# The last four heads' keys turned to token rows behind the last output product

## The chip, the cores and the metric

The kernel runs on one core of a Trainium2 chip. The metric is the device time of one execution in microseconds; the time before is 2034.35 us, the median of three runs (2033.86 to 2036.96).

A core has five engines with instruction streams of their own: PE (TensorE) multiplies matrices and transposes, with results in PSUM banks; DVE (VectorE), ACT (ScalarE) and POOL (GpSimd) work on elements; SP (SyncE) does little but issue transfers, which 16 DMA engines carry out. Each engine takes its instructions in order. They wait for each other by semaphores.

## The reference

One step of a hybrid decoder layer. A normalised input `h` (16 meta tokens, 1024 tokens of a prompt, 32 tokens of eight samples: 1072 rows) is multiplied by one wide matrix. Its parts feed eight heads of attention (the change calls it softmax attention; the weights are made by breaking a stick) and a gated linear attention, and both go through one output product, a norm and a residual. Beside the two `y`, the new keys and values are outputs, by token:

```python
h = rms_norm(x, norm_pre_g[l])
(q, k, v), sg, (gq, gk, gv, gf), gg = branch_inputs(h, w_in[l], w_alpha[l], b_alpha[l])
o_sb = sb_prompt(q, k, v, sb_bias[l])
o_gla, s_end = gla_prompt(gq, gk, gv, gf)
x = x + rms_norm(branch_output(o_sb, sg, o_gla, gg, gla_norm_g[l], w_out[l]), norm_post_g[l])
k_p.append(k)
```

`new_k_prompt` is 1040 tokens x 8 heads x 128 features, `new_k_sample` 32 tokens x 8 heads x 128. One token's key of one head is a run of 512 bytes, and the next token's lies 4 KB further on.

## The kernel before

The input product is made by feature: 128 features of one head in the partitions, the 1072 tokens along the row, in three chunks of 384, 384 and 304 columns (`CHUNKS`, L40). All products are made of float32 split in two parts, three matmuls for one (L347 to L349). For each head, `head(h)` (L721) makes values, keys and queries, in this order, while the attention of the head before runs between them (`attend`, L689). A `Weaver` (L58) interleaves such pieces of work: a piece is a generator that is resumed after a number of beats, and the products call `W.beat()`. A scheduler then sets the order on each engine; with `tc.add_manual_dep(..., NOSYNC, reason="behind")` the kernel asks that one instruction stands behind another, with no wait.

A chunk of keys leaves PSUM in `ev_k` (L761): ACT copies it to `raw`, `split_k` makes the two parts for the attention, and `tok_out` (L548) makes token rows: three PE transposes to a bank (L556), a copy by ACT to `st` (L558 to L561), and a store from SP to the outputs (L564; for the last chunk also L566 and L567).

The output stage (L1361) works on the 1024 prompt tokens in two halves of 512 by a scheme with seven products (`p`), each for two column blocks (`q`). The last one, `p` 4 with `q` 1, runs token tile by token tile (L1744 to L1750, four tiles of 128 tokens): `before_last`, eight steps of `product` (L1679) on weights kept in SBUF, `take_last` (L1561; sum on DVE, square on ACT), and `finish1` (L1658), which makes the root and the four blocks of 512 columns of the tile's rows. `end_block` (L1648) scales, adds the input and stores from SP. For tile 3, one block goes by ACT and POOL and is stored by ACT (L1676), and block 1 is stored in two halves. The names in the views: `u` is block 0, `y` blocks 2 and 3, `og` block 1. `finish_samples` (L1630) does the 32 sample rows beside it (`held`: eight stores of 32 KB, L1646).

At this point the slots of region C (`REGION`, L1401; 10 to 13 of the 16 long slots) have held the forms of product 7 and are free, and so are the slots of the ring of weights (4 and 5). `bank` (L1513) deals six PSUM banks in turn; two more have the tag `S`. Transfers tell of their landing by eight semaphores, `DMAHW0` to `DMAHW7`, dealt in turn to the DMAs of SP and ACT together; a DMA waits until the one that had its semaphore before has landed.

Of the kernel before, what the change touches and what calls it, by code (L numbers as in the profile page):

```python
# [10 lines left out]
F32 = mybir.dt.float32  # L11
# [4 lines left out]
AF = mybir.ActivationFunctionType  # L16
# [4 lines left out]
P = 128  # L21
# [7 lines left out]
T = META + SEQ + NSMP  # L29
REAL = META + SEQ  # L30
TOUT = SEQ + NSMP
HEADS = 8
# [19 lines left out]
IDLE = -1000000  # L52

EB = 4 * P
NOSYNC = mybir.DependencyInfo(mybir.DependencyClass.NoSync, mybir.DependencyReason.DATA)


# [32 lines left out]
def hybrid_step(ctx: ExitStack, tc: tile.TileContext, x_prompt, x_sample, cache_k, cache_v, state_gla,  # L90
# [3 lines left out]
    nc = tc.nc  # L94
    mm = nc.tensor.matmul
    vec, act, pool = nc.vector, nc.scalar, nc.gpsimd
# [13 lines left out]
    dram = ctx.enter_context(tc.tile_pool(name="dram", bufs=1, space=DRAM))  # L110
# [3 lines left out]
    W = Weaver()  # L114
# [5 lines left out]
    ident = cst.tile([P, P], F32, name="ident")  # L120
# [33 lines left out]
    zd = [dram.tile([P, 256], F32, name=f"zd{b}") for b in range(NB)]  # L154
    od = [dram.tile([P, TOUT], F32, name=f"od{g}") for g in range(NK)]
    md = [dram.tile([P, TOUT], F32, name=f"md{g}") for g in range(NK)]
    znd = dram.tile([NSMP, HEADS, NSMP], F32, name="znd")
    td = [dram.tile([P, 8, 1024], F32, name=f"td{j}") for j in range(4)]
    sd = [[dram.tile([P, 512], F32, name=f"sd{j}_{k}") for k in range(8)] for j in range(2)]
# [35 lines left out]
    with tc.tile_pool(name="xp", bufs=2) as xp, tc.tile_pool(name="xps", bufs=5, space=PSUM) as xps:  # L195
        wf = xp.tile([P, 12, P], F32R, tag="wf", bufs=1, name="wf")
        wfl = [stg.tile([P, 2, P], F32R, tag="stg", name=f"wfl{kk}") for kk in range(6)]
        first = [accp.tile([P, 512], F32, tag="acc", name=f"acc_v0_{c}") for c in range(3)]
# [106 lines left out]
        for c, (lo, hi) in enumerate(XCHUNKS):  # L305
            n = hi - lo
# [173 lines left out]
    def spread(ins):  # L480

        if W.mark is not None:
            tc.add_manual_dep(ins.ins, W.mark.name, NOSYNC, reason="spread")

# [53 lines left out]
    with tc.tile_pool(name="sp", bufs=1) as sp, tc.tile_pool(name="sps", bufs=1, space=PSUM) as sps:  # L538
# [9 lines left out]
        def tok_out(raw, c, lo, hi, h, outp, outs_, nm):  # L548

            yield 6  # L550
            os_ = outs_[0].rearrange("b t h d -> (b t) h d")
            ps = sps.tile([P, 512], F32, tag="z", bufs=4, name=f"tk_{nm}_{c}")
            st = stage(f"st_{nm}_{c}")
            for i in range(3):
                r = min(P, hi - lo - i * P)
                nc.tensor.transpose(ps[:r, i * P:(i + 1) * P], raw[:, i * P:i * P + r], ident[:])  # L556
            if c < 2:
                act.copy(st[:], ps[:, :384])  # L558
            else:
                act.copy(st[:, :256], ps[:, :256])  # L560
                act.copy(st[:48, 256:], ps[:48, 256:384])  # L561
            sv = st[:].rearrange("p (a d) -> p a d", d=P)
            nt = 3 if c < 2 else 2
            nc.sync.dma_start(outp[0, 0, lo:lo + nt * P, h, :].rearrange("(a p) d -> p a d", p=P), sv[:, :nt])  # L564
            if c == 2:
                nc.sync.dma_start(outp[0, 0, 8 * P:REAL, h, :], sv[:16, 2, :])  # L566
                nc.sync.dma_start(os_[:, h, :], sv[16:48, 2, :])  # L567
# [153 lines left out]
        def head(h):  # L721
# [39 lines left out]
            def ev_k(c, ps, lo, hi):  # L761
                raw = stage(f"kraw{h}_{c}")
                act.copy(raw[:, :hi - lo], ps)
                W.spawn(split_k(raw, c, lo, hi))
                W.spawn(tok_out(raw, c, lo, hi, h, new_k_prompt, new_k_sample, f"k{h}"))
            inproj(C_SK + h * P, ev_k, 0, f"k{h}")
            qt = [sp.tile([P, SEQ], F32R, tag=f"q{i}", name=f"q{i}_{h}") for i in range(2)]
            qsm = sp.tile([P, NSMP], F32, tag="qsm", name=f"qsm{h}")
# [28 lines left out]
    with tc.tile_pool(name="gp", bufs=1) as gp, tc.tile_pool(name="gps", bufs=1, space=PSUM) as gps:  # L797
# [20 lines left out]
        def slot(c):  # L818

            return 8 if c == 8 else 4 * (1 - c % 2) + c // 2  # L820
# [540 lines left out]
    with ExitStack() as out:  # L1361
# [151 lines left out]
        def bank(nm):  # L1513
            n = next(at) % 6
            return accp.tile([P, 512], F32, tag="acc", name=nm) if n < 3 else ops.tile([P, 512], F32, tag="m", bufs=3, name=nm)
# [114 lines left out]
        def finish_samples():  # L1630
            yield 5
            ps = ops.tile([P, 512], F32, tag="S", bufs=2, name="tsp")
            tot = op.tile([P, 4], F32, tag="tot", name="tots")
            vec.tensor_tensor(tot[:, 1:2], sssm[:, 0:1], sssm[:, 1:2], ALU.add)
            mm(ps[:, 0:1], rep, tot[:, 1:2], start=True, stop=True)
            vec.tensor_copy(tot[:, 0:1], ps[:, 0:1])
            r = rstd_(op, tot[:, 0:1], D, P, 1, "ys")
            xv = x_sample.rearrange("b t d -> (b t) d")
            yv = y_sample.rearrange("b t d -> (b t) d")
            for i in range(2):  # L1640
                x = stage(f"xs_{i}")[:, :256]
                for j in range(4):
                    nc.sync.dma_start(x[32 * j:32 * j + 32], xv[:, i * 1024 + j * 256:i * 1024 + (j + 1) * 256])
                vec.scalar_tensor_tensor(ysm[i][:], ysm[i][:], r, x, ALU.mult, ALU.add)
                for j in range(4):
                    nc.sync.dma_start(yv[:, i * 1024 + j * 256:i * 1024 + (j + 1) * 256], ysm[i][32 * j:32 * j + 32])  # L1646

        def end_block(i, b, r, behind=None):  # L1648
            o = scaled[i][:] if b == 1 else sums_[4 + i, b]
            w = 256 if b == 1 and i == 3 else 512  # L1650
            for c0 in range(0, 512, w):
                cs, ys = slice(c0, c0 + w), slice(b * 512 + c0, b * 512 + c0 + w)
                ins = vec.scalar_tensor_tensor(o[:, cs], o[:, cs], r, xr[i, b][:, cs], ALU.mult, ALU.add).ins
                if behind is not None:
                    tc.add_manual_dep(ins, behind.name, NOSYNC, reason="behind")
                nc.sync.dma_start(y_prompt[0, 512 + i * P:512 + (i + 1) * P, ys], o[:, cs])

        def finish1(i, v):  # L1658
            rt = op.tile([P, 12], F32, tag="rs", name=f"rt_y{i}")
            r, t = rt[:, 0:1], rt[:, 1:2]  # L1660
            act.activation(r, v, AF.Ln)
            act.activation(r, r, AF.Exp, scale=-0.5)
            vec.scalar_tensor_tensor(t, r, v, r, ALU.mult, ALU.mult)
            vec.tensor_scalar(t, t, -0.5, 1.5, ALU.mult, ALU.add)
            vec.tensor_tensor(r, r, t, ALU.mult)
            if i == 3:
                o = sums_[7, 2]
                act.activation(o, o, AF.Copy, scale=r)
                pool.tensor_tensor(o, o, xr[3, 2], ALU.add)
            for b in (0, 3) if i > 1 else (0, 2, 3, 1):  # L1670
                end_block(i, b, r)
            if i == 2:
                end_block(i, 2, r)
                return lambda behind: end_block(i, 1, r, behind)
            if i == 3:
                nc.scalar.dma_start(y_prompt[0, 512 + 3 * P:, 1024:1536], o)  # L1676
                end_block(i, 1, r)
# [53 lines left out]
        for pair in ((1, 2), (6,), (5, 3), (7, 4)):  # L1731
            for q in range(2):
                banks = [bank(f"b{pair[0]}{q}_{t}") for t in range(4)]
                for p in pair:
# [3 lines left out]
                    if (p, q) != (4, 1):  # L1738
                        step(p, q, banks, p == pair[0], p == pair[-1])
                        AFTER.get((p, q), lambda: None)()  # L1740
        W.spawn(finish_samples())

        scaled, rest = {}, None
        for t in range(4):  # L1744
            tot = before_last(t)
            for k in range(8):
                product(banks[t], t, 4, k, kept[k], False, True)
                W.beat()
            take_last(t, banks[t], tot, rest)
            rest = finish1(t, tot[:, 1:2])  # L1750
        W.flush()


# [27 lines left out]
```

## Time and profile before

| | us |
|---|---|
| median of three runs | 2034.35 |
| the profiled execution | 2034.71 |
| its span, first to last instruction | 2033.0 |
| PE busy | 2004.2 |
| DVE busy | 1496.9 |
| ACT busy | 1018.4 |
| PE, transposes of keys `tk_k` (L556), 72 of 272 ns | 93.8 to 731.5 |
| last product of PE starts | 2023.1 |

The profile is of one execution. Its times are from the first instruction on; "start us, us" in a timeline are start and duration. Matmuls are pipelined: the next one starts before the one before has ended, so what a matmul costs in a stream is the distance between starts, not its duration. A row of the table by stretches has, in order: the stretch, its length, busy us of PE, PEld, DVE, ACT and POOL with the number of instructions, the granted clock of PE, the share of time in which the DMA engines are busy, and GB/s.

### The profile page before, as it was taken

The numbers are of one execution on the slowest core, as the hardware profiler recorded it, in microseconds if no ns is written. First come the engines' busy times: TensorE is split into PE (matmuls) and PEld (weight loads), VectorE is DVE, ScalarE is ACT, GpSimd is POOL, SyncE is SP. The second block draws the span as 40 slices with busy tenths as digits, with TensorE's granted clock in tenths as the row PEclk, the third lists the DMA queues.
The fourth block names the chain that finished last, engine by engine and source line by source line (L and its number), as shares of the span: only waits on it lengthen the run. The fifth ranks groups of instructions, "written<-read, shape, count | busy, mean of one in ns | idle before, by whom it ended". The sixth has DMA issues, their size and how long they took to land.

```text
span 2033.0 us, 41746 instructions
## 1 busy us (share of the span) xinstructions
PE 2004.2 (99%) x12379; PEld 1852.4 (91%) x12379; DVE 1496.9 (74%) x6163; ACT 1018.4 (50%) x2377; POOL 96.1 (5%) x355
## 2 busy tenths in 40 slices
PE   6999999999999999999999999999999999999998
PEld 5999999999999999999999999999988898788776
DVE  7368888888888888899898888978444338365466
ACT  7356767675766757433535335254433335343342
POOL 0111110101000010000000000000000000000000
PEclk9999999999999999999999999999999999999999
DMA  6345554545555442433342434335767656352485
GB/s 205 98 136 161 143 163 132 175 129 157 151 161 151 141 125 77 142 101 89 103 108 80 126 79 120 90 93 176 243 220 234 221 186 221 104 176 94 141 281 204
DMA packets 371980, 301.92 MB, mean 149 GB/s; under 512 B 42336, under 2 KB 312264, under 8 KB 371752
## 3 DMA queue, kind: packets, MB, share of 16 engines
q1 hardware_dynamic: 371448, 298.73, 49.1%
q8 instruction: 97, 1.59, 0.3%
q14 instruction: 131, 1.07, 0.2%
q10 hardware_dynamic: 304, 0.53, 0.1%
HBM read 241.84 MB, written 57.31 MB: 147 GB/s over the span
## 4 chain that ended last, share of the span: by engine, by line
PE 91%; DVE 3%; DMA 2%; ACT 2%; issue 1%; SPq 0%; DVEq 0%; POOL 0%; POOLq 0%; ACTq 0%
PE acc_g L347 6%; PE acc_g L348 5%; PE acc_g L349 5%; PE b L1682 4%; PE b L1683 4%; PE b L1684 4%; PE acc_gv L347 3%; PE acc_gv L348 3%; PE acc_gv L349 3%; PE acc_k L347 3%; PE acc_k L349 3%; PE acc_k L348 3%; PE acc_q L348 3%; PE acc_q L347 3%; PE acc_q L349 3%; PE acc_v L347 3%
## 5 line engine op out<-in xcount | busy, mean ns | idle before, releaser
L470 DVE SCALAR_TENSOR_TENSOR jk<-kp,qb 128x128 f32<-128x128 f32 x2048 | 593.6, 290 | 46.2 <-DMA qb<-qsd 3.0
L347 PE MATMUL acc_g<-hT,wh_g 128*128 128x368 f32 (+2 forms) x768 | 250.7, 326 | 0.0
L348 PE MATMUL acc_g<-hT,wh_g 128*128 128x368 f32 (+2 forms) x768 | 247.2, 322 | 0.0
L349 PE MATMUL acc_g<-hT,wl_g 128*128 128x368 f32 (+2 forms) x768 | 246.9, 321 | 0.0
L470 DVE DVE_READ_ACCUMULATOR jk<-kp,qb 128x1 f32 x2048 | 167.3, 82 | 0.0
L1682 PE MATMUL b<-ring,f 128*128 128x512 f32 x416 | 163.9, 394 | 1.5 <-DVE y L1547 1.1
L1683 PE MATMUL b<-ring,f 128*128 128x512 f32 x416 | 162.3, 390 | 0.0
L1684 PE MATMUL b<-ring,f 128*128 128x512 f32 x416 | 161.9, 389 | 0.0
L347 PEld LDWEIGHTS acc_g<-hT,wh_g 128*128 128x128 f32 x768 | 144.3, 188 | 12.0 <-issue 10.7
L348 PEld LDWEIGHTS acc_g<-hT,wh_g 128*128 128x128 f32 x768 | 144.4, 188 | 0.7
L349 PEld LDWEIGHTS acc_g<-hT,wl_g 128*128 128x128 f32 x768 | 144.2, 188 | 0.0
L1481 DVE TENSOR_TENSOR ring<-wr,ring 128x512 fp32r<-128x512 f32 x104 | 71.2, 689 | 97.7 <-ACT ring L1480 97.1
L1480 ACT CAST ring<-wr 128x512 fp32r<-128x512 f32 x104 | 64.0, 620 | 134.7 <-PE b L1684 78.1
L347 PE MATMUL acc_gv<-hT,wh_gv 128*128 128x402 f32 (+2 forms) x384 | 130.1, 339 | 0.0
L347 PE MATMUL acc_k<-hT,wh_k 128*128 128x384 f32 (+1 forms) x384 | 126.1, 328 | 0.0
L348 PE MATMUL acc_gv<-hT,wh_gv 128*128 128x402 f32 (+2 forms) x384 | 125.3, 326 | 0.0
L349 PE MATMUL acc_gv<-hT,wl_gv 128*128 128x402 f32 (+2 forms) x384 | 125.0, 326 | 0.0
L349 PE MATMUL acc_k<-hT,wl_k 128*128 128x384 f32 (+1 forms) x384 | 124.7, 325 | 0.0
L348 PE MATMUL acc_k<-hT,wh_k 128*128 128x384 f32 (+1 forms) x384 | 124.4, 324 | 0.0
L347 PE MATMUL acc_q<-hT,wh_q 128*128 128x368 f32 (+2 forms) x384 | 124.3, 324 | 0.0
L348 PE MATMUL acc_q<-hT,wh_q 128*128 128x368 f32 (+2 forms) x384 | 123.6, 322 | 0.0
L349 PE MATMUL acc_q<-hT,wl_q 128*128 128x368 f32 (+2 forms) x384 | 123.3, 321 | 0.0
(483 smaller groups left out, 5263.6 us busy)
## 6 DMA issues: line engine op xcount, KB each, us to landing
kp<-in_cache_k_dram SPq DMA_DIRECT2D x512, 64.0 KB
vr<-in_cache_v_dram SPq DMA_DIRECT2D x64, 512.0 KB
qb<-qsd SPq DMA_DIRECT2D x64, 256.0 KB
wr_g<-in_w_in_dram SPq DMA_DIRECT2D x64, 256.0 KB
wr<-td SPq DMA_DIRECT2D x56, 256.0 KB
tf<-in_w_out_dram SPq DMA_DIRECT2D x48, 256.0 KB
td<-tf SPq DMA_DIRECT2D x48, 256.0 KB
wr<-in_w_out_dram SPq DMA_DIRECT2D x48, 256.0 KB
```

Source lines behind the costliest of these rows:

```text
L347: mm(acc[c][:, :n], wh, hh[k][:, lo:hi], start=(k == 0), stop=False)
L348: mm(acc[c][:, :n], wh, hl[k][:, lo:hi], start=False, stop=False)
L349: W.mark = mm(acc[c][:, :n], wl, hh[k][:, lo:hi], start=False, stop=(k == NK - 1)).ins
L470: ins = vec.scalar_tensor_tensor(jk[:], kp[:], 1.0, qbs[h, b][:, t, :], ALU.mult, ALU.mult, accum_out=zt[:, t, NPG - 1 - i:NPG - i])
L1480: act.copy(wh, r)
L1481: vec.tensor_tensor(wl, r, wh.bitcast(F32), ALU.subtract)
L1682: mm(bk[:], ah, wh, start=first and k == 0, stop=False, skip_group_check=True)
L1683: mm(bk[:], ah, wl, start=False, stop=False, skip_group_check=True)
L1684: W.mark = mm(bk[:], al, wh, start=False, stop=last and k == 7, skip_group_check=True).ins
```

## The change

For heads 4 to 7 (`LATE` is 4) `ev_k` no longer starts `tok_out`. It stores `raw` as it is, by feature, to a scratch `kd` in DRAM (3 stores a head, 128 rows of 1536 or 1216 bytes). Behind the weights of the output stage, `load_late` brings the four heads back, 128 x 1072 each, to two slots of region C. `late_rows` then makes the token rows: nine banks `kb0` to `kb8` of four transposes each, two banks for a head's 1024 first tokens, and the ninth for the last 48 tokens of all four heads; all of them stand behind the last product. ACT copies six of the banks and DVE three (5, 6 and 8, behind the last block of `y`) to `kst`. SP stores a head's 1024 tokens in one DMA of 512 KB, and the last 48 tokens in two. The order on SP around the last tile's stores is asked for by hand.

```diff
+LATE = HEADS - 4
+    kd = [dram.tile([P, T], F32, name=f"kd{i}") for i in range(4)]
...
-                W.spawn(tok_out(raw, c, lo, hi, h, new_k_prompt, new_k_sample, f"k{h}"))
+                if h < LATE:
+                    W.spawn(tok_out(raw, c, lo, hi, h, new_k_prompt, new_k_sample, f"k{h}"))
+                else:
+                    nc.sync.dma_start(kd[h - LATE][:, lo:hi], raw[:, :hi - lo])
...
-                nc.sync.dma_start(y_prompt[0, 512 + i * P:512 + (i + 1) * P, ys], o[:, cs])
+                ends[:] = [ins]
+                stores.append(nc.sync.dma_start(y_prompt[0, 512 + i * P:512 + (i + 1) * P, ys], o[:, cs]).ins)
...
-            act.activation(r, r, AF.Exp, scale=-0.5)
+            tail[:] = [act.activation(r, r, AF.Exp, scale=-0.5).ins]
...
-                act.activation(o, o, AF.Copy, scale=r)
+                tail.append(act.activation(o, o, AF.Copy, scale=r).ins)
...
+        kr = [slot(REGION["C"][i], f"kr{i}") for i in range(2)]
+        kf = [kr[j // 2][:, j % 2 * T:(j % 2 + 1) * T].bitcast(F32) for j in range(4)]
+        kst = [slot(REGION["C"][2 + i], f"kst{i}") for i in range(2)]
+
+        def load_late():
+            for j in range(4):
+                yield 4
+                spread(nc.sync.dma_start(kf[j], kd[j][:]))
+
+        def late_rows():
+            last = W.mark
+            for n in range(9):
+                ps = ops.tile([P, 512], F32, tag="S", bufs=2, name=f"kb{n}") if n in (2, 3) else bank(f"kb{n}")
+                rows = P if n < 8 else T - 8 * P
+                for i in range(4):
+                    src = kf[n // 2][:, (n % 2 * 4 + i) * P:(n % 2 * 4 + i + 1) * P] if n < 8 else kf[i][:, 8 * P:T]
+                    ins = nc.tensor.transpose(ps[:rows, i * P:(i + 1) * P], src, ident[:]).ins
+                    tc.add_manual_dep(ins, last.name, NOSYNC, reason="behind")
+                st = (kst[n // 4][:, n % 4 * 512:(n % 4 + 1) * 512] if n < 8 else slot(4, "kst2")[:, 0:512]).bitcast(F32)[:rows]
+                if n in (5, 6, 8):
+                    ins, first = vec.tensor_copy(st, ps[:rows, :]).ins, ends[0]
+                else:
+                    ins, first = act.copy(st, ps[:rows, :]).ins, (last, *tail)[min(n, 2)]
+                tc.add_manual_dep(ins, first.name, NOSYNC, reason="behind")
+                if n == 8:
+                    sv = st.rearrange("p (h d) -> p h d", d=P)
+                    nc.sync.dma_start(new_k_prompt[0, 0, 8 * P:REAL, LATE:HEADS, :], sv[:16])
+                    nc.sync.dma_start(new_k_sample[0].rearrange("b t h d -> (b t) h d")[:, LATE:HEADS, :], sv[16:48])
+                elif n % 2:
+                    sv = kst[n // 4][:, n % 4 * 512 - 512:n % 4 * 512 + 512].bitcast(F32)
+                    ins = nc.sync.dma_start(new_k_prompt[0, 0, :1024, LATE + n // 2, :].rearrange("(a p) d -> p a d", p=P),
+                                            sv.rearrange("p (a d) -> p a d", d=P)).ins
+                    for a, b in {1: ((stores[-4], ins), (stores[-3], stores[-4])),
+                                 3: ((ins, stores[-3]), (stores[-2], ins), (stores[-1], stores[-2]))}.get(n, ()):
+                        tc.add_manual_dep(a, b.name, NOSYNC, reason="behind")
+
+        W.spawn(load_late())
...
+        late_rows()
```

Three places in the built programs. First SP, at the stores of tiles 0 and 1. Before (`u_0`, `y_0_0`, `y_1_0` and the first `og` are tile 0's; the second digit of `y` is the tile):

```order
L1656 DMA out_dram<-u_0_29289 128x512
L1656 DMA out_dram<-y_0_0_30310 128x512
L1646 DMA out_dram<-held_29114 32x256 x4
L1646 DMA out_dram<-held_29115 32x256 x4
L1656 DMA out_dram<-y_1_0_30627 128x512
L1656 DMA out_dram<-og_31518 128x512
L1656 DMA out_dram<-u_1_29291 128x512
```

And now, with the loads `kr`:

```order
L1651 DMA out_dram<-held_29034 32x256 x4
L1651 DMA out_dram<-held_29035 32x256 x4
L1664 DMA out_dram<-u_0_29209 128x512
L1664 DMA out_dram<-y_0_0_30230 128x512
L1664 DMA out_dram<-y_1_0_30547 128x512
L1664 DMA out_dram<-og_31443 128x512
L1757 DMA kr_31359<-kd_125 128x1072
L1757 DMA kr_31360<-kd_126 128x1072
L1664 DMA out_dram<-u_1_29211 128x512
```

All eight sample stores have moved ahead of tile 0's rows, and two loads stand between tiles 0 and 1; one more stands behind tile 1's `og`, and the first one further ahead. Second, DVE at the same place, the work that fills these stores. Before:

```order
L1653 SCALAR_TENSOR_TENSOR y_0_0_30310<-y_0_0_30310,rt_y_31523,xr_0_2_31448 128x512
L1644 SCALAR_TENSOR_TENSOR held_29114<-held_29114,vrt_ys,xs_31486 128x256
L1644 SCALAR_TENSOR_TENSOR held_29115<-held_29115,vrt_ys,xs_31496 128x256
L1653 SCALAR_TENSOR_TENSOR y_1_0_30627<-y_1_0_30627,rt_y_31523,xr_0_3_31453 128x512
L1566 TENSOR_TENSOR u_1_29641<-b_1_31239,u_1_29641 128x512
L1653 SCALAR_TENSOR_TENSOR og_31518<-og_31518,rt_y_31523,xrs_31158 128x512
```

And now:

```order
L1660 SCALAR_TENSOR_TENSOR y_0_0_30230<-y_0_0_30230,rt_y_31448,xr_0_2_31372 128x512
L1649 SCALAR_TENSOR_TENSOR held_29034<-held_29034,vrt_ys,xs_31411 128x256
L1660 SCALAR_TENSOR_TENSOR y_1_0_30547<-y_1_0_30547,rt_y_31448,xr_0_3_31377 128x512
L1660 SCALAR_TENSOR_TENSOR og_31443<-og_31443,rt_y_31448,xrs_31078 128x512
L1571 TENSOR_TENSOR u_1_29561<-b_1_31159,u_1_29561 128x512
L1649 SCALAR_TENSOR_TENSOR held_29035<-held_29035,vrt_ys,xs_31421 128x256
```

The second half of the sample rows has moved behind three instructions of 512 columns. Third, the end of the program, with the semaphores that each row waits for. SP before, from the last block of tile 2 on:

```order
L1656 DMA out_dram<-og_31610 128x512 [waits DMAHW6_49,DVE_49]
L1656 DMA out_dram<-u_3_29295 128x512 [waits DMAHW7_49,DVE_49]
L1656 DMA out_dram<-y_1_3_30633 128x512 [waits DMAHW1_49,DVE_49]
L1656 DMA out_dram<-og_31654 128x256 [waits DMAHW2_49,DVE_49]
L1656 DMA out_dram<-og_31654 128x256 [waits DMAHW3_49,DVE_49]
```

And now:

```order
L1664 DMA out_dram<-og_31538 128x512 [waits DMAHW3_49,DVE_49]
L1780 DMA out_dram<-kst_31361 128x8x128 [waits DMAHW4_49,Activation_49]
L1664 DMA out_dram<-u_3_29215 128x512 [waits DMAHW5_49,DVE_49]
L1664 DMA out_dram<-y_1_3_30553 128x512 [waits DMAHW6_49,DVE_49]
L1780 DMA out_dram<-kst_31361 128x8x128 [waits DMAHW7_49,Activation_49]
L1664 DMA out_dram<-og_31582 128x256 [waits DMAHW0_49,DVE_49]
L1664 DMA out_dram<-og_31582 128x256 [waits DMAHW1_49,DVE_49]
L1780 DMA out_dram<-kst_31362 128x8x128 [waits DMAHW2_49,DVE_49,Activation_49]
L1780 DMA out_dram<-kst_31362 128x8x128 [waits DMAHW3_49,DVE_49,Activation_49]
L1776 DMA out_dram<-kst_31663 16x512 [waits DMAHW4_49,DVE_49]
L1777 DMA out_dram<-kst_31663 32x512 [waits DMAHW5_49]
```

ACT there, now (`kb` are the banks with transposes, `b_3` is tile 3's bank):

```order
L1772 COPY kst_31361<-kb_31606 128x512 [waits PE_49]
L1573 ACTIVATE b_3_31161,held_29035<-u_3_29565 128x512 [waits DVE_49]
L1669 ACTIVATE rt_y_31589<-part_31555 128x1 [waits DVE_49]
L1670 ACTIVATE rt_y_31589<-rt_y_31589 128x1 [waits Activation_49]
L1772 COPY kst_31361<-kb_31612 128x512 [waits PE_49]
L1676 ACTIVATE y_0_3_30236<-y_0_3_30236,rt_y_31589 128x512 [waits DVE_49]
L1772 COPY kst_31361<-kb_31619 128x512 [waits PE_49]
L1772 COPY kst_31361<-kb_31625 128x512 [waits PE_49]
L1684 DMA out_dram<-y_0_3_30236 128x512 [waits DMAHW0_49,Pool_49]
L1772 COPY kst_31362<-kb_31632 128x512 [waits PE_49]
L1772 COPY kst_31362<-kb_31651 128x512 [waits PE_49]
```

The stores of heads stand between tile 3's on SP, and copies of banks between the square, the root and the store of tile 3 on ACT. Of the landing semaphores, `DMAHW0` was ACT's alone among these rows before (its store waits for `DMAHW0` too); now ACT's store and the first half of `og` behind it on SP have it one after the other.

More of the change, by code (lines that the diff above doesn't have):

```diff
@@ L1646, in finish_samples @@
                     nc.sync.dma_start(yv[:, i * 1024 + j * 256:i * 1024 + (j + 1) * 256], ysm[i][32 * j:32 * j + 32])
+        tail, ends, stores = [], [], []
         def end_block(i, b, r, behind=None):
```

## The prediction

> **What bounds the kernel now.** I read the page first, then the lines of the transposes that move, then the end of the program.
>
> ```profile
> span 2033.0 us, 41746 instructions
> PE 2004.2 (99%) x12379; PEld 1852.4 (91%) x12379; DVE 1496.9 (74%) x6163; ACT 1018.4 (50%) x2377; POOL 96.1 (5%) x355
> PE 91%; DVE 3%; DMA 2%; ACT 2%; issue 1%; SPq 0%; DVEq 0%; POOL 0%; POOLq 0%; ACTq 0%
> ```
>
> The third line is the chain that ended last: 91% of the span is PE. So PE time that goes out of the stream should shorten the run one for one, as long as nothing is late behind it. The page leaves the end to be looked at by itself. The chain of waits gives it, in order of time (start, us, what):
>
> ```profile
> 2023.23 0.24 PE b L1684
> 2023.49 0.70 DVE u L1566
> 2024.22 0.73 ACT b L1568 x2
> 2026.28 0.75 DVE u L1653
> 2027.69 1.80 DVE og L1653 x2
> ```
>
> The last product ends at 2023.47; then tile 3 is normalised and stored, and PE has nothing to do for 9.5 us. The issues of SP and ACT there, from the timeline:
>
> ```profile
> 2011.71 3.65 SPq L1646 DMA_DIRECT2D out_dram<-held  x8
> 2015.46 0.37 SPq L1656 DMA_DIRECT2D out_dram<-y  x1
> 2018.54 0.33 SPq L1656 DMA_DIRECT2D out_dram<-og  x1
> 2021.99 0.33 SPq L1656 DMA_DIRECT2D out_dram<-u  x1
> 2024.87 0.33 SPq L1656 DMA_DIRECT2D out_dram<-og  x1
> 2027.06 0.33 SPq L1656 DMA_DIRECT2D out_dram<-u  x1
> 2028.84 0.38 ACTq L1676 DMA_DIRECT2D out_dram<-y  x1
> 2029.12 0.83 SPq L1656 DMA_DIRECT2D out_dram<-og  x2
> ```
>
> And the table by stretches; its last two columns are the share of time in which the 16 DMA engines are busy, and GB/s:
>
> ```profile
> 77.00:78.00 1.00, 1.00 (x8) 1.00 (x8) 0.00 (x0) 0.00 (x0) 0.00 (x0) 1.00 1.15 342
> 459.00:460.00 1.00, 1.00 (x8) 1.00 (x7) 1.00 (x4) 0.71 (x3) 0.00 (x0) 1.00 0.95 286
> 1470.00:1471.50 1.50, 1.50 (x13) 1.50 (x12) 0.15 (x1) 0.00 (x0) 0.00 (x0) 1.00 1.04 418
> 2016.50:2020.00 3.50, 3.50 (x17) 2.92 (x16) 3.40 (x7) 0.73 (x2) 0.00 (x0) 1.00 1.01 380
> 2020.50:2022.50 2.00, 2.00 (x11) 1.65 (x10) 1.82 (x5) 0.04 (x1) 0.00 (x0) 1.00 0.01 2
> 2022.00:2022.80 0.80, 0.80 (x5) 0.68 (x4) 0.80 (x2) 0.00 (x0) 0.00 (x0) 1.00 0.00 0
> 2022.80:2023.00 0.20, 0.20 (x2) 0.16 (x2) 0.20 (x1) 0.00 (x0) 0.00 (x0) 1.00 0.83 328
> 2031.40:2033.00 1.60, 0.00 (x0) 0.00 (x0) 0.00 (x0) 0.00 (x0) 0.00 (x0) 0.50 0.00 0
> ```
>
> The reader is to see that the DMA engines are full from 2016.5 to 2020, while the stores of two tiles drain, and empty from 2020.5. A store issued at 2021.99 moves data from about 2022.85, 0.9 us later. The last byte is out by 2031.35, and 1.65 us later the span ends. The 2.3 us without data (2020.5 to 2022.8) and some shorter pauses between later stores are all the room that the end has for other transfers.
>
> **What the change removes.** Twelve groups of three transposes leave the stream of PE. Two of them, with their neighbours:
>
> ```profile
> 728.39 0.49 PE L556 MATMUL tk_k<-ident,kraw 128*128 128x128 f32 x3
> 728.64 0.42 PE L347 MATMUL acc_q<-hT,wh_q 128*128 128x384 f32 x1
> 728.89 0.33 PE L348 MATMUL acc_q<-hT,wh_q 128*128 128x384 f32 x1
> 729.07 0.33 PE L349 MATMUL acc_q<-hT,wl_q 128*128 128x384 f32 x1
> 731.29 0.49 PE L556 MATMUL tk_k<-ident,kraw 128*128 128x128 f32 x3
> 731.54 0.37 PE L680 MATMUL O<-hi_a,V 128*128 128x276 f32 x1
> ```
>
> Starts are what counts in a pipelined stream. A group holds PE for 0.25 us (728.39 to 728.64, 731.29 to 731.54). In the first, the matmul behind it also takes 0.25 to the next start, where its like takes 0.18 (728.89 to 729.07): 0.08 more. One group of each head stands before such a matmul, the others before ones that start slowly anyway. So a head gives 3 x 0.25 + 0.08 = 0.83, and four heads **3.3 us**. I bound it by 3.0 (no extra at all) and 4.0 (0.08 at every group).
>
> ```profile
> L558 ACT COPY st_k<-tk_k x16: 449/462/482, 94.5 to 730.5; 128x384 f32<-128x384 f32 x16
> 458.03 2.27 SPq L564 DMA_DIRECT2D out_dram<-st_k  x3
> ```
>
> The evacuations that leave (0.46 us and less, 12 groups) and SP's five stores a head, now three, I cost at nothing: ACT is busy half the span, and PE covers both. If that cover were thin, the new order of SP in heads 4 to 7 could stall PE; that is a rival below.
>
> **What it adds, on the old clock.** I keep the times of the old trace and take the 3.3 us off at the end. 36 transposes now start when the last product does its last rows, at 2023.3. Nine in a row go one every 0.10:
>
> ```profile
> 72.77 1.14 PE L556 MATMUL tk_v<-ident,vraw 128*128 128x128 f32 x9
> 73.66 0.42 PE L347 MATMUL acc_k<-hT,wh_k 128*128 128x384 f32 x1
> L1529 ACT COPY u<-b x8: 577/588/608, 1718.7 to 1767.8; 128x512 f32<-128x512 f32 x8
> 2027.14 1.68 POOL L1669 TENSOR_TENSOR y<-y,xr 128x512 f32<-128x512 f32 x1 [324.50 <-DMA out_dram<-og]
> ```
>
> 36 take 3.6 us and lie in PE's idle end: nothing. Of the nine evacuations (0.59 each by L1529) the first stands on ACT ahead of tile 3's square. Its bank is ready near 2023.9, it ends at 2024.5, and the square moves from 2024.22 by 0.25; the second fits behind the root. So tile 3's chain is 0.25 late, the first block of rows is whole at 2026.4, and ACT's store, behind POOL's 1.68, goes at 2029.1. None of it counts if the DMA engines are behind by then. That is the point.
>
> SP's order decides when they are. The two sets of sample stores now stand ahead of tile 0's four stores, and the second set behind tile 1's sum on DVE:
>
> ```profile
> 2011.16 0.88 DVE L1644 SCALAR_TENSOR_TENSOR held<-held,vrt_ys,xs 128x256 f32<-128x256 f32 x2
> 2012.62 0.69 DVE L1566 TENSOR_TENSOR u<-b,u 128x512 f32<-128x512 f32 x1
> ```
>
> On DVE the second half comes after y, og and u, done at 2014.0 and not 2012.0; its four stores (3.65 / 8 = 0.46 each) end at 2015.9. Only then come tile 0's four, two loads, tile 1's four and a load, each 0.4 of SP. Data run from 2016.8, at 0.4 asked for against 0.69 served, so the queue fills at once. From there the DMA engines have to move:
>
> - 16 stores of 256 KB (four a tile), 2 KB a row, at 380 GB/s: 16 x 0.69 = 11.0 us
> - 3 loads of a head, 549 KB, in rows of 4 KB, at 418 (a page of values, 1470 to 1471.5): 3 x 1.31 = 3.9
> - 4 stores of a head, 524 KB, in rows of 512 B, at 286 (459 to 460, when SP's three stores of st_k alone are moving): 4 x 1.83 = 7.3
> - 48 rows of 2 KB: 0.3
>
> Together 22.6 us, from 2016.8 to 2039.4. It doesn't pause: by 2020.5 SP has asked for 9.4 us of it (busy to 2026.2), tile 2 carries it to 2029.0, and the first head's store is issued at 2026.45. Add 1.65: 2041.05; less 3.3: a span of 2037.7, **4.7 us more**. The profiled execution took 2034.71, so 2039.4; it lies 0.36 above the median of the runs (2034.35), so I write 2039.0 for the median.
>
> The term that the trace shows least is the head's store, 4 x 1.83. Its ends are 342 GB/s (77 to 78, with loads of 512 B among the stores: 1.53) and 250 (2.1, if several segments a partition drain worse than these three); I take 286, the nearest. The twelve stores to the scratch (0.55 MB a head) and the first head's load stand in stretches with DMA to spare: nothing.
>
> By the Trainium skill, "DMA: Bandwidth & Descriptors", Specifications, 512 B is enough for the line rate. By that rule a head's store would cost no more per byte than the tiles' rows, 1.38 us, and the sum would be 2.9 and not 4.7. The trace disagrees: 286 GB/s at a share of 0.95, against 380 at 1.01.
>
> **Rivals.**
> - *Rows of 512 B drain faster*, because loads and stores overlap (share 1.15, 342 GB/s at 77 to 78), at 342 or up to the 380 of long rows. It decides the sign of the verdict: 8.04 MB at a mean of 356 GB/s is my forecast, and from 366 on (a head's store in 1.68) the change is not slower by 0.2%. At 1.53 it gives 2037.8, at 1.38 2037.2, with loads beside stores 0.5 us better still: 2036.0 to 2037.8, at 2037.2. For it: that share. Against it: the pure stores at 459.
> - *No queue at all*, SP's issue ends it: DVE's last three evacuations follow og (2029.5 + 0.25, then 3 x 0.65), so the last small store is issued at 2032.1, and it is 3.4 us to the end as now (second og 2029.55 to 2033.0): 2035.5 less 3.3, so 2033.6. It needs 476 GB/s; the best row is 418.
> - *A new wait on SP.* og of tile 3 shares a landing semaphore with ACT's store of y and so waits for it to land; behind og on SP stand its second half, two heads and the small rows. How long a landing takes to be known, the waits of SP's queue tell (us in total, times, longest):
>
> ```profile
> SPq L1770 <- DMA out_dram<-og: 1.9, 2, 1.5
> ```
>
> SP's last issue ends at 2029.95 and its two waits for og last 1.9, to 2031.9, 0.6 behind the last byte. If ACT's 256 KB lies behind everything asked for before, it moves at 2034.1 to 2034.7, is known at 2035.3, and og's first data come at 2036.3: 1.6 us of idle DMA, 2040.6. If it is served in between, it lands by 2032 and costs nothing. The Trainium skill, "DMA: Bandwidth & Descriptors", Queues, rings and completion order, says that an engine goes round the queues that have work; by that this rival falls. No row here shows both queues full.
> - *The early saving doesn't come*, since SP's new order in heads 4 to 7 makes PE wait: 4.7 + 3.3, 2042.4. Against it: PE's idle time before tk_k and its neighbours is nil there.
>
> **How the numbers follow.** About 0.2% (4.1 us) is what a measurement of this kernel can tell from no change: slower begins at 2038.4, faster ends at 2030.3. Forecast 0.50 (own range 2037.6 to 2040.2, two thirds of it above 2038.4), faster rows 0.22, no queue 0.08, new wait 0.13, no saving 0.07. Slower: 0.33 + 0.13 + 0.07, some of it given up for rates that mix, 0.52. Same: 0.17 + 0.22 + 0.08, 0.46 with what is left; faster needs more than the whole saving: 0.02. The range leaves out no queue and no saving: 2035.0 to 2041.3.
>
> **What would show it.** Right: head to head, heads 4 to 7 take 0.8 us less each, and the last product ends 3.3 earlier (2020.2); DMA share near 1 without a pause from the first store of tile 0 to about 1.7 us before the end; a head's store moves in 1.8 us; the stretch from the last product to the end is 17.5 us, not 9.5. Wrong: a pause in DMA after 2016 of the old clock (SP or an engine ends it), heads' rows at 340 or more, a long wait of SP ahead of og of tile 3, or a stall of PE in heads 4 to 7. If the whole end is 13 us or less, the queue was never there.

## The result, and the profile after

| | before | changed |
|---|---|---|
| median of nine runs, us | 2034.19 (2033.63 to 2036.96) | 2040.63 (2039.43 to 2041.29) |
| profiled execution, us | 2034.71 | 2041.27 |
| its span, us | 2033.0 | 2039.5 |
| end of the last product, us | 2023.5 | 2020.9 |
| from there to the end of the span, us | 9.5 | 18.6 |

The ratio is 1.0029, with an interval of [1.0021, 1.0037]: 6 us slower. It lies inside the predicted range (2035.0 to 2041.3), 1.6 above the predicted time, and above the range of the forecast by itself (2037.6 to 2040.2). PE does end earlier, by 2.6 us; the end grows by 9.1.

The page of the changed kernel, its length and the chain that ended last:

```profile
span 2039.5 us, 41740 instructions
PE 2005.1 (98%) x12379; PEld 1851.8 (91%) x12379; DVE 1497.9 (73%) x6166; ACT 1016.4 (50%) x2367; POOL 94.8 (5%) x355
PE 87%; DVE 5%; DMA 3%; ACT 2%; issue 1%; SPq 1%; POOL 0%; DVEq 0%; ACTq 0%; POOLq 0%
```

PE is busy for as long as before (the transposes are done all the same); its part of the chain falls from 91% to 87%, and DVE's and DMA's grow. Its timeline where PE's last product ends (start, us, engine, line, what; the transposes `kb` follow at once):

```profile
2020.50 0.40 PE L1692 MATMUL b<-keep,f 128*128 128x512 f32 x1
2020.73 0.49 PE L1766 MATMUL kb<-ident,kr 128*128 128x128 f32 x3
```

And its table by stretches for the end, with the columns as in the table of before (the last two are the share of time in which the DMA engines are busy, and GB/s):

```profile
2014.50:2016.50 2.00, 2.00 (x11) 1.65 (x10) 2.00 (x4) 0.00 (x0) 0.00 (x0) 1.00 1.00 376
2018.00:2021.00 3.00, 3.00 (x16) 2.47 (x15) 2.65 (x7) 0.00 (x0) 0.00 (x0) 1.00 0.92 277
2021.50:2023.00 1.50, 1.28 (x11) 0.91 (x10) 1.17 (x4) 1.27 (x4) 0.00 (x0) 1.00 1.05 405
2027.50:2029.50 2.00, 2.00 (x10) 1.46 (x8) 0.93 (x2) 0.58 (x1) 0.00 (x0) 0.50 1.12 364
2033.50:2037.00 3.50, 0.00 (x0) 0.00 (x0) 0.00 (x0) 0.00 (x0) 0.00 (x0) 0.50 0.96 299
2037.80:2039.50 1.70, 0.00 (x0) 0.00 (x0) 0.00 (x0) 0.00 (x0) 0.00 (x0) 0.50 0.01 4
```

The share is 0.92 or more in every one of them up to 2037, 16 us after the last product, while before it fell to 0.01 ahead of tile 3's rows. The loads of keys (2018 to 2021) move at 277 GB/s, the heads' stores by themselves (from 2033.5) at 299. The last data is out near 2037.8, and 1.7 us later the span ends, as before.

Two lists of waits hold the rest. PE's in heads 4 to 7 (380 to 740 us; what waited, for whom, us in total, times, longest), before and then changed:

```profile
PE z L654 <- DVE lo_s L599: 0.3, 1, 0.3
```

```profile
PE z L655 <- ACT hi_s L598: 2.2, 4, 0.8
```

Once in each head PE now waits for `hi_s`. And SP's from 2012 us on:

```profile
SPq L1664 <- DMA out_dram<-y: 3.3, 2, 3.0
SPq L1664 <- DMA kr<-kd: 2.3, 2, 1.7
```

SP stands for 3.0 us ahead of tile 3's `og`, until ACT's store of `y` has landed: the wait of the third rival. PE has a wait there too, from 2020 us on:

```profile
PE kb L1766 <- DMA kr<-kd: 3.0, 1, 3.0
```

The last load of keys is asked for at 2019.82 and known to have landed near 2027; only then do the last twelve transposes start. What that costs is a question for b1_loads_early.

### The profile page after: what moved, and what is told of

Read it like the earlier page. It is cut to its first block, busy times and chain, and to the rows that moved or that the text cites. A ratio compares the mean times of both kernels' runs of the same rounds, so it can differ in the third digit from the quotient of the medians.

```text
span 2039.5 us, 41740 instructions
## 1 busy us (share of the span) xinstructions
PE 2005.1 (98%) x12379; PEld 1851.8 (91%) x12379; DVE 1497.9 (73%) x6166; ACT 1016.4 (50%) x2367; POOL 94.8 (5%) x355
## 4 chain that ended last, share of the span: by engine, by line
PE 87%; DVE 5%; DMA 3%; ACT 2%; issue 1%; SPq 1%; POOL 0%; DVEq 0%; ACTq 0%; POOLq 0%
PE acc_g L349 6%; PE acc_g L350 5%; PE acc_g L351 5%; PE b L1690 4%; PE b L1691 4%; PE b L1692 4%; PE acc_gv L349 3%; PE acc_gv L350 3%; PE acc_gv L351 3%; PE acc_k L349 3%; PE acc_k L351 3%; PE acc_k L350 3%; PE acc_v L349 3%; PE acc_v L350 3%; PE acc_v L351 3%; PE acc_q L350 2%
```

## The experiments

Every ratio is to runs of the kernel before on the same chip. Their median was 2034.19 beside the changed kernel, 2035.69 beside a1 to a4, 2035.27 beside b0 to b3, 2034.99 beside c1 and c2, and 2036.06 beside c3 and c4; so the ratio is the number to read, and medians only within one of these groups. The interval of each ratio is about 0.0009 to either side (0.0012 for b0). The last two columns are of the one profiled execution: where its timeline has the end of the last product, and from there to the end of its span. That execution can differ from the median of its run, most in c1 (1.5 faster) and c2 (2.2 slower).

| run | median | ratio | last product | to the end |
|---|---|---|---|---|
| before | 2034.19 | 1 | 2023.5 | 9.5 |
| changed | 2040.63 | 1.0029 | 2020.9 | 18.6 |
| a1_no_late_rows | 2032.45 | 0.9985 | 2020.1 | 9.5 |
| a2_z_later | 2039.74 | 1.0019 | 2019.2 | 18.8 |
| a3_og_free | 2040.95 | 1.0022 | 2021.3 | 18.7 |
| a4_no_head_stores | 2036.89 | 1.0004 | 2021.3 | 14.0 |
| b0_changed_again | 2041.28 | 1.0033 | 2020.5 | 18.8 |
| b1_loads_early | 2039.24 | 1.0023 | 2020.4 | 16.4 |
| b2_rows_2k | 2038.73 | 1.0018 | 2020.2 | 16.0 |
| b3_all_three | 2036.86 | 1.0009 | 2018.9 | 15.9 |
| c1_all_og_free | 2035.56 | 0.9999 | 2018.3 | 14.1 |
| c2_two_heads | 2036.35 | 1.0006 | 2024.7 | 12.1 |
| c3_four_heads_best | 2033.89 | 0.9994 | 2017.1 | 13.9 |
| c4_two_heads_best | 2036.11 | 1.0001 | 2023.2 | 11.4 |

**The saving alone.** The theory after the result: the end is a drain of the DMA engines, and part of the saving is lost to `hi_s`. The first run leaves the end as it was.

```diff
-        W.spawn(load_late())
...
-        late_rows()
```

> The loads, transposes and stores behind the last product are left out, so the keys of heads 4 to 7 are written to the scratch and not to the outputs. What stays is the saving in heads 4 to 7 alone. The forecast's step (0.83 a head, all of it kept): 2034.2 - 3.3 = 2030.9, the last product at 2020.2 or so. The theory from the trace of the changed kernel, in which PE waits 2.2 us in four places for hi_s where it waited 0.5 before: the saving is 1.5 to 2.6, so 2031.6 to 2032.7, with the last product of PE at 2020.5 to 2021.5 and the four waits still there. A rival that puts all of the loss in heads 4 to 7: 2034.2 or more.

Ratio 0.9985 [0.9976, 0.9994], some 3 us less than the kernel before, and the end is 9.5 us again. By the ratio the forecast's 3.3 and the other theory's 1.5 to 2.6 cannot be told apart. The trace can: the four waits are there without any work behind the last product.

```profile
PE z L655 <- ACT hi_s L598: 2.2, 4, 0.9
```

(The list of before, above, has one wait of 0.3 in their place, not the 0.5 of the expectation.) From head 4's first product of values to the first of the gates, heads 4 to 7 take 383.1 us in the kernel before (386.90 to 769.98 in its timeline) and 381.9 here (386.64 to 768.49): 1.2 saved.

**The wait for hi_s.** What stands there is shown by the timeline of the changed kernel:

```profile
460.24 0.30 PE L351 MATMUL acc_q<-hT,wl_q 128*128 128x304 f32 x1
460.38 0.33 PE L349 MATMUL acc_q<-hT,wh_q 128*128 128x368 f32 x1
460.88 0.62 ACT L598 CAST hi_s<-X 128x512 fp32r<-128x512 f32 x1
461.55 0.50 PE L655 MATMUL z<-hi_s,ntri 128*128 128x512 f32 x1 [0.84 <-ACT hi_s L598]
```

and of the kernel before:

```profile
461.08 0.62 ACT L596 CAST hi_s<-X 128x512 fp32r<-128x512 f32 x1 [0.24 <-POOL X L626]
461.51 0.30 PE L349 MATMUL acc_q<-hT,wl_q 128*128 128x304 f32 x1
461.75 0.50 PE L653 MATMUL z<-hi_s,ntri 128*128 128x512 f32 x1
```

The chain of DVE, POOL and ACT that makes `hi_s` is no faster (0.2 us earlier), and PE, without the transposes, is at `z` 1.1 us earlier (0.3 of that is a lead that PE has from ahead of head 4). The next run puts this product of the attention's last tile one beat later where the next head's keys are late:

```diff
-            yield D1 if n > 300 or h == HEADS - 1 else D1 - 1
+            yield D1 + 1 if qi == 0 and j == 0 and LATE <= h + 1 < HEADS else D1 if n > 300 or h == HEADS - 1 else D1 - 1
```

> The changed kernel, with the product that waits for hi_s (the last tile of the attention, which runs in the next head's queries) put one beat later in heads 4 to 7, so that five matmuls of the queries stand ahead of it. If the removed transposes were what covered hi_s, the four waits go (2.2 us) and the last product ends 1.5 to 2.2 earlier. Whether the time follows depends on the end: if the DMA engines start on tile 0's rows earlier by the same, 2040.6 - 1.9 = 2038.7; if the drain is held by something else, 2040.6. If the wait only moves to the next product of the chain (lo_s, or the output product), nothing changes.

2039.74, a ratio of 1.0019 [1.001, 1.0028]. The wait falls to

```profile
PE z L656 <- DVE lo_s L601: 0.9, 2, 0.6
```

and the last product ends 1.7 us earlier than in the changed kernel, with the end about as long as there (18.8 and 18.6). Heads 4 to 7 take 381.8 us in the changed kernel (386.63 to 768.39) and 380.4 in this one (386.69 to 767.11): 1.3 and 2.7 saved, of 3.3. The time follows by 1.5 us in the profiled executions (spans of 2039.5 and 2038.0); the intervals of the two ratios overlap, so the medians alone don't show it.

**The new wait on SP.** ACT's block of tile 3 is stored by SP, behind the second head:

```diff
-                nc.scalar.dma_start(y_prompt[0, 512 + 3 * P:, 1024:1536], o)
+                byact.append(nc.sync.dma_start(y_prompt[0, 512 + 3 * P:, 1024:1536], o).ins)
...
-                                 3: ((ins, stores[-3]), (stores[-2], ins), (stores[-1], stores[-2]))}.get(n, ()):
+                                 3: ((ins, stores[-3]), (byact[0], ins), (stores[-2], byact[0]), (stores[-1], stores[-2]))}.get(n, ()):
```

> The changed kernel, with the one block of tile 3 that ACT stores now stored by SP, behind the second head's store; og of tile 3 then has a landing semaphore that was free 5 us before, so the 3.0 us in which SP waited for that store to land are gone, and heads 2 and 3 are asked for some 3 us earlier. If the DMA engines' queue sets the end (share 1.0 throughout in the trace), the same bytes in another order: 2040.6, within 0.5. If the new wait sets it, up to 3.0 less: 2037.6 to 2039.0.

2040.95, a ratio of 1.0022 [1.0013, 1.0031], and an end of 18.7 us: nothing that is clear of the noise, although of SP's waits for `y` only 0.5 us is left, in two places. While the DMA engines had work asked for, it did not matter when SP asked for more.

**The heads' stores.** The four stores of 512 KB are left out, so the first 1024 tokens' keys of heads 4 to 7 aren't written.

```diff
-                    ins = nc.sync.dma_start(new_k_prompt[0, 0, :1024, LATE + n // 2, :].rearrange("(a p) d -> p a d", p=P),
-                                            sv.rearrange("p (a d) -> p a d", d=P)).ins
```

> The changed kernel without the four stores of 512 KB (the first 1024 tokens' keys of heads 4 to 7 are made and copied, and not written to the outputs); loads, transposes and copies stay. If the end is a drain of the DMA engines, it loses what these four cost in it: 4 x 1.83 by the forecast, 2033.3; by the mixed rate of the trace after 2027.5 (about 350 GB/s, 1.5 each) 2034.6. If engines or SP's issues set the end (transposes behind the loads, DVE's last copies at 2030.3, small rows behind them), 2038 to 2040.

2036.89, ratio 1.0004 [0.9995, 1.0013]. Its table by stretches:

```profile
2022.00:2030.50 8.50, 5.11 (x30) 3.92 (x28) 6.45 (x14) 4.73 (x11) 1.67 (x1) 0.75 1.05 404
2030.70:2033.00 2.30, 0.00 (x0) 0.00 (x0) 0.44 (x1) 0.00 (x0) 0.00 (x0) 0.50 0.17 56
```

The drain is over near 2030.7, 9.4 us behind the last product, where it took 16.9 in the changed kernel (2037.8 less 2020.9): the stores cost some 7.5 in the drain, near the forecast's 7.3. Yet the end is only 4.6 shorter. SP's list says why:

```profile
SPq L1776 <- DMA out_dram<-y: 3.3, 1, 3.3
```

Here it is the small rows that share ACT's semaphore, and wait 3.3 us with the DMA engines nearly idle. So none of the expected times came: the term was right, and what comes next was not foreseen.

**Loads earlier.** The four loads stand together behind the loads of the sample rows, and the stores of sample rows (collected in `heldst`) behind them:

```diff
-            for j in range(4):
-                yield 4
-                spread(nc.sync.dma_start(kf[j], kd[j][:]))
+            yield 5
+            for j in range(4):
+                ins = nc.sync.dma_start(kf[j], kd[j][:])
+                spread(ins)
+                for s_ in heldst:
+                    tc.add_manual_dep(s_, ins.ins.name, NOSYNC, reason="behind")
```

> The changed kernel once more, as the base of the runs beside it: 2040.6, a ratio of 1.003 to the kernel before.

> The changed kernel, with all four loads of heads 4 to 7 issued right behind the loads of the sample rows (near 2006), ahead of the stores of the sample rows, where the DMA engines are mostly idle up to 2014. Theory of the drain: three loads, 5.2 us of the 16 engines' time in the trace from 2014 on, leave the drain; one load or so of it comes back, as the four take 7 to 8 us from 2006.5 and so delay tile 0's stores by up to 0.7: 4.5 less than the changed kernel, 2036.1. If the end hung on the order of SP or on an engine, 2039.5 to 2041. If four loads ahead of the sample rows' stores hold up SP (its stores wait for landing semaphores of the loads), 2038.

The changed kernel came out at 2041.28 (ratio 1.0033), and this one at 2039.24: 2.0 less, not 4.5. So the late load that PE waited for in the changed kernel, and the bytes of the loads in the drain, were together worth no more than that here. The table by stretches of b1_loads_early:

```profile
2006.70:2012.00 5.30, 5.30 (x25) 4.39 (x24) 4.87 (x11) 1.09 (x4) 0.00 (x0) 1.00 0.97 384
2023.00:2024.00 1.00, 1.00 (x12) 0.98 (x11) 0.90 (x4) 0.80 (x2) 0.00 (x0) 1.00 0.50 184
2031.00:2034.50 3.50, 0.00 (x0) 0.00 (x0) 0.00 (x0) 0.00 (x0) 0.00 (x0) 0.50 0.92 282
```

The loads did go into the idle time. But a shorter queue runs dry: a pause at 2023, where SP waits 1.0 us for the copy of the second bank, and at the end the heads' rows of 512 B alone, at 282 GB/s, with nothing beside them.

**Rows of 2 KB.** A bank now takes one tile of tokens of all four heads, on top of the early loads:

```diff
-                    src = kf[n // 2][:, (n % 2 * 4 + i) * P:(n % 2 * 4 + i + 1) * P] if n < 8 else kf[i][:, 8 * P:T]
+                    src = kf[i][:, n * P:n * P + rows]
...
-                    ins = nc.sync.dma_start(new_k_prompt[0, 0, :1024, LATE + n // 2, :].rearrange("(a p) d -> p a d", p=P),
+                    ins = nc.sync.dma_start(new_k_prompt[0, 0, (n - 1) * P:(n + 1) * P, LATE:HEADS, :].rearrange("(a p) h d -> p a (h d)", p=P),
```

> As the run with early loads, and each bank now takes one tile of 128 tokens of all four heads, so that a row of the store holds four heads' features of one token, 2 KB and not 512 B; the same bytes, the same number of transposes, copies and stores. By the forecast's rates (1.83 a head against 1.38) 1.8 less than the run with early loads; by the packets of the changed kernel's trace (4096 of 27 ns against 1024 of 86 ns on 16 engines: 6.9 against 5.5) 1.4 less: 2034.5. If rows of 512 B cost no more per byte, no difference.

2038.73, only 0.5 less, which the intervals do not tell from nothing. The rows do move faster, 379 GB/s (tile 2's rows and the keys', all of 2 KB) against 282, but the table by stretches of b2_rows_2k has a hole in it, and SP's list has the reason:

```profile
2024.00:2028.50 4.50, 0.15 (x2) 0.00 (x0) 4.25 (x6) 2.00 (x4) 1.67 (x1) 0.91 1.01 379
2028.80:2030.30 1.50, 0.00 (x0) 0.00 (x0) 0.00 (x0) 0.00 (x0) 0.00 (x0) 0.50 0.03 10
```

```profile
SPq L1666 <- DMA out_dram<-y: 3.7, 1, 3.7
```

The wait that cost nothing in the changed kernel now leaves the DMA engines without work for 1.5 us. With the edit of a2_z_later added:

> As the run with early loads and rows of 2 KB, and the product that waits for hi_s one beat later in heads 4 to 7. PE ends some 1.6 earlier, as in the run with that edit alone. If the drain starts earlier by the same, 2032.9, which would beat both kernels; if the drain now starts only when the loads are out (they stand ahead of tile 0's stores), half of it: 2033.7. If an engine's chain behind the last product ends it (DVE's last copies, then the small rows, 3.4 to the end), the gain still passes through: 2033.

2036.86, 1.9 less than b2_rows_2k: the last product ends 1.4 earlier in the profile, and the end is the same (15.9 and 16.0). The expected times (2032.9 to 2033.7) are missed by 3 to 4 us, since b2_rows_2k had already come out 4 above its own.

**The wait again, now with a short queue.** b3_all_three with the edit of a3_og_free:

> The run with all three edits, and tile 3's block of ACT stored by SP behind the second store of keys, as in the run a3_og_free, where that gave nothing. With the DMA queue shorter, the trace of b2_rows_2k shows what was hidden before: the DMA engines idle from 2028.8 to 2030.4 while SP waits for ACT's store to land ahead of og. If that wait now costs, 1.5 to 2.0 less than b3_all_three: 2035.1, level with the kernel before. If the drain still sets the end, no change: 2036.9.

Ratio 0.9999 [0.9991, 1.0008]; the end falls from 15.9 to 14.1, and the hole is gone:

```profile
2022.00:2030.50 8.50, 0.23 (x3) 0.00 (x0) 4.32 (x7) 1.98 (x5) 1.68 (x1) 0.77 1.01 372
```

The same edit gave nothing to the changed kernel and 1.8 us of the end here. The ratio falls by 0.001, 2 us, and the two intervals overlap; it is the hole in the trace that shows the cause.

**Toward a version that beats both.** With two late heads and not four, the same edits, the small rows first, the keys' stores ahead of `og`, and all banks copied by ACT:

```diff
-LATE = HEADS - 4
+LATE = HEADS - 2
```

> Two late heads (6 and 7) and not four, with early loads, rows of 1 KB, the product behind hi_s one beat later, SP storing all of tile 3, the 48 last tokens first, and the keys' stores ahead of og. Half of the saving (1.7 to 1.8 with the wait for hi_s gone) and 1.1 MB in the end, 3.0 us of the DMA engines against the 3.5 us that they were idle between 2016.5 and 2031.4 in the kernel before. Theory of the drain: the end grows by 0.3 to 0.9 (the copy ahead of tile 3's square, SP's issues), so 0.9 to 1.4 less than the kernel before, which beats both. If stores of keys only fit behind the last rows of y, the end grows by 3: 1.2 more than before.

Ratio 1.0006 [0.9998, 1.0015]; the gain that was expected did not come. The time is near the expectation's other case (1.2 more), but not by its sum: in the profiled execution, a slow one for this run, the end is 2.6 longer than before, and the last product is not earlier but 1.2 later. Then sample rows in two stores instead of eight, the first store of keys split by bank (with two heads, every store), and `z` two beats later in the last of the heads, for four heads and for two:

```diff
-                for j in range(4):
-                    nc.sync.dma_start(yv[:, i * 1024 + j * 256:i * 1024 + (j + 1) * 256], ysm[i][32 * j:32 * j + 32])
+                heldst.append(nc.sync.dma_start(yv[:, i * 1024:(i + 1) * 1024].rearrange("t (j c) -> j t c", j=4), ysm[i][:]).ins)
```

> As c1_all_og_free, with what its trace left: the eight stores of sample rows (3.7 us of SP's issue ahead of tile 0's rows, DMA engines at a share of 0.13 to 0.65 for 2 us) as two, the first store of keys split by bank so that its first half goes out before tile 3's first block (share 0.33 there), and the product behind hi_s two beats later in the last head (0.9 us of wait left). Theory of the drain: these 1.3 and 0.7 us of idle DMA and up to 0.5 of PE come off: 2033.1 to 2034.0, a ratio of 0.9990 to 0.9995. If the end is now set by SP's issues behind the last product, no change: 2035.5, 1.0000.

> As c2_two_heads, with the same: sample rows in two stores, the keys' stores one for each bank, two beats in the last head. In c2_two_heads the end was 12.1 us behind the last product, with the DMA engines idle for 1.7 us of it (2026 to 2029) and at 0.25 for 4 us before tile 0's rows. With both gone the end is 10 to 10.5 behind it and the saving is 1.7: 0.8 to 1.2 less than the kernel before, a ratio of 0.9994 to 0.9996, and 2 less than c2_two_heads. If the saving of two heads does not reach the last product (it ended later than in the kernel before), 1.0000 or more.

Four heads: 2033.89 against 2036.06 of the kernel before, a ratio of 0.9994 [0.9985, 1.0003], the lowest of all that write every output, and not clear of the kernel before. Its list of waits in heads 4 to 7 is down to that of the kernel before:

```profile
PE z L656 <- DVE lo_s L601: 0.3, 1, 0.3
```

and those heads take 379.5 us (386.80 to 766.26), with the 36 transposes gone and nothing else: 3.6 saved, where the forecast had 3.3. Two heads: 1.0001 [0.9992, 1.001], no gain. Both runs with two heads end the last product late for the same reason, a wait in the output stage that is 1.1 us in the kernel before and 0.3 in c3_four_heads_best; of c4_two_heads_best:

```profile
PE b L1694 <- DVE y L1553: 3.3, 1, 3.3
```

In c4_two_heads_best the heads do give the 1.7 that was expected (381.35 us, 386.43 to 767.78), and this wait, 2.2 longer than in the kernel before, takes nearly all of it back. Why DVE is later there was not followed up, so how many late heads would be best stays open.

## Why the prediction was right, and where it was off

- **The time.** The forecast by itself reached up to 2040.2, and 2040.63 is above that; it is inside the whole range only because that had to hold the rivals too. It is also, to a tenth, the time of the third rival (2040.6), whose wait came and cost nothing: that agreement is chance. What the runs show is the forecast's mechanism, a drain, with the saving forecast too large and the drain too short.
- **PE bounds the run, and time off PE shortens it.** Right: a1_no_late_rows has the end of before and is faster; in a2_z_later a last product 1.7 earlier makes a span 1.5 shorter.
- **3.3 us saved.** Too much, and this is the step that was off: heads 4 to 7 gave 1.3. The price of the transposes was right; c3_four_heads_best, with no more wait than before, saves 3.6. The prediction weighed each group of transposes by the distance between starts, found PE without idle time around them and looked for a wait on SP. It did not ask what else was hidden by them. They were the filler ahead of `z`, whose `hi_s` comes from a chain of other engines; the wait of 0.3 for `lo_s` in the list of before was a sign that this product had little slack. So the fourth rival's effect came in part, by another mechanism. With the product moved, 2.7 of the 3.3 are there, and 0.9 of wait is left. (The last product is 2.6 earlier in the profile; some 1.0 of that is a wait of PE in the gated stage, `acc_gk` for ACT, which the profile of before has and this one hasn't. In a1_no_late_rows it is 3.3 earlier, the forecast's figure, and that is luck: heads 4 to 7 gave 1.2 of it, and the same wait is gone.)
- **The end is a drain.** Right. Forecast: data from 2013.5 to 2036.1, 22.6 us, without a pause. Seen: 2014.2 to 2037.8, 23.6, or 8.04 MB at a mean of 341 GB/s where the forecast had 356. It starts 0.7 later, as PE is 0.7 later than forecast at the last product, and takes 1.0 longer; together 1.7 of the 1.8 by which the span exceeds the forecast (2039.5 against 2037.7). Tile 3 is 0.2 late, near the 0.25 of the forecast: its first rows start on DVE 3.0 us behind the last product, 2.8 before.
- **The terms of the drain.** Stores of a head: 7.3 by the forecast, some 7.5 by a4_no_head_stores. Loads were mis-sized: priced at 418 GB/s, they moved at 277 where they ran alone, so two of them took 2 x 549 KB / 277 = 4.0 us and not 2.6; that is 1.3, a little more than the drain's excess of 1.0. In b2_rows_2k the same loads, four in a row, move at 401 once under way, so the rate isn't one of their shape. The 36 transposes were priced at nothing, as if they ran in one go; they did cost nothing in the changed kernel, but the last twelve had to wait for a load.
- **Rows of 512 B faster** (first rival): for half of the stores. The last two heads' moved at 299 GB/s, and those of b1_loads_early at 282: the forecast's 286. (The 250 at the other end of the forecast has no row behind it, and no stretch shown here is that slow.) The first two heads', however, moved as the rival had it, here in two stretches in which nearly all packets are such rows (in the second, 489 of 506 are under 2 KB):

```profile
2028.20:2029.20 1.00, 1.00 (x7) 0.76 (x5) 0.42 (x1) 0.42 (x1) 0.00 (x0) 0.50 1.14 353
2031.70:2032.50 0.80, 0.00 (x0) 0.00 (x0) 0.00 (x0) 0.00 (x0) 0.00 (x0) 0.50 1.14 355
```

  That is the prediction's sign of being wrong (340 or more). The rival's reason, loads beside the stores, isn't there: the last load had landed near 2027. By these rates the four stores take 6.5 us (two at 354, two at 299); by leaving them out, a4_no_head_stores gives some 7.5. Why these sums differ, and why two heads' rows move faster than the other two's, stays open. By the Trainium skill, "DMA: Bandwidth & Descriptors", Specifications, 512 B reach the line rate. Alone, these rows reach 74 to 80% of what rows of 2 KB do (376 to 379), and in the two stretches 93 to 94%.
- **No queue, ended by SP's issue** (second rival): no; the share says so, and a3_og_free.
- **The new wait on SP** (third rival): it came, 3.0 us long, and cost nothing, since the DMA engines had 3 us of work asked for. The prediction priced it at 1.6 of idle DMA; b2_rows_2k shows 1.5, once the queue is short, and c1_all_og_free gets 1.8 back. The Trainium skill, "DMA: Bandwidth & Descriptors", Queues, rings and completion order, has an engine go round the queues that have work, by which ACT's block would have been served between SP's. The trace speaks against it here. The DMA view of the changed kernel has, for 2027 to 2029 and then for 2029 to 2031, by queue (packets, MB, share):

```profile
q1 hardware_dynamic: 913, 0.74, 109.0%
```

```profile
q1 hardware_dynamic: 531, 0.53, 75.2%
q10 hardware_dynamic: 143, 0.26, 34.0%
```

  ACT asked for its store at 2026.49 and SP's queue, q1, is all that moves until 2029; ACT's queue, q10, has its 256 KB in the next two. It was not served in between, but behind what SP had asked for earlier. Where it was held, the trace doesn't show.

## What to carry to other kernels

Instructions that are taken out of a full engine's stream may have been the cover of somebody's latency: look at the next product that waits for another engine, and move it back by as much. That took the saving here from 1.3 to 2.7 and, with one more beat in the last head, to 3.6. Work that is moved into an engine's idle end is free on that engine alone; add up its bytes at the rates of the rows there, and see whether the DMA engines were idle too. A wait that costs nothing behind a full queue is not harmless: when the queue is shortened, it can be the next limit, so a cause that is undone by itself can look worth nothing (a3_og_free) and be worth 1.8 us behind another (c1_all_og_free).

## What the runs showed of the hardware

- Loads of 549 KB in rows of 4 KB moved at 277 GB/s between stores (share 0.92) and at 401 as four in a row:

```profile
2006.70:2011.70 5.00, 5.00 (x24) 4.14 (x23) 4.70 (x10) 0.95 (x4) 0.00 (x0) 1.00 0.99 401
```

  (b2_rows_2k; in the 0.7 us ahead of that stretch, while they start, it is 112). What slows the former was not tried by itself.
- Stores in rows of 512 B moved at 282 to 299 GB/s at shares of 0.92 to 0.96, and at 353 and 355 at a share of 1.14; rows of 2 KB, in the stretches shown, at 372 to 380 at shares of 1.00 to 1.01.
- A store asked for by ACT at 2026.49 moved nothing until 2029, behind those that SP had asked for before, in a queue of its own.
- Landing semaphores dealt in turn to the DMAs of two engines tie SP to a store that another engine issued: 3.0, 3.3 and 3.7 us of waiting in three kernels, each time of whatever store had the same semaphore.
